# The last two column tiles of an output projection computed side by side, with the first gate weights and the seventh pair of forms prepared among their steps

## The chip, the cores and the metric

The kernel runs on one core of one Trainium2 chip. The metric is device microseconds of one execution, the median of several runs. The engines of the core are named as in the profile: PE (TensorE, the matrix unit; PEld is its loading of the stationary operand), DVE (VectorE), ACT (ScalarE), POOL (GpSimd), SP (SyncE, which here only issues transfers). Each engine has its own queue of instructions and works it off in the order in which the program was built; engines wait for each other with semaphores. A transfer (DMA) is issued by an instruction in one of these queues.

## The reference

One layer of a hybrid decoder on 512 positions of width 2048, all in float32: a norm, one input projection, eight heads of forgetting attention and eight of a compressed, selected and sliding-window attention, then an output projection with a residual, a second norm and a SwiGLU block with a residual. What matters for this change is the seam between two of these:

```
o = concatenate([o_fox, o_nsa], axis=-1) @ w_out       # 512x2048 @ 2048x2048
x = x + o                                              # x1 below
h = _rms_norm(x, ffn_norm)
x = x + (silu(h @ w_gate) * (h @ w_up)) @ w_down       # inner width 5632
```

## The kernel before, in words

All is kept transposed: a tile holds 128 of the 2048 columns on its partitions, and the 512 positions along the free axis. A float32 product is made of three products of a faster type: each operand is split into a high part (a rounded copy, made by ScalarE, line 82) and a low part (the rest, made by VectorE, line 79), and `mm3` (lines 170 to 172) adds high x high, high x low and low x high into the same bank of PSUM. The third of these needs the weights' low part; the first two need only the high one.

**The output projection.** There are 16 column tiles, in the order m = 0 to 15; tile m holds columns n = m // 2 + 8 (m % 2), so two tiles in a row are the halves of one pair. Each needs the 16 tiles `om` of the attention's result (`bigm`, two parts each) as moving operand, and 2 x 1024 columns of weights. `gemm_steps` takes them in two halves: load (`ws`, three buffers), split into high and low (`wp`, two buffers), eight steps of three matmuls. `gemm2` does two tiles at once from the same moving operand: four quarters of weights, and in each four steps of 2 x 3 matmuls. Before the change only tiles 0 and 1 go through `gemm2`.

**What follows each tile** is `x1_steps`: load the tile of x (`xr`), add the projection to it (DVE, into `x1`), store x1 in DRAM (issued by ACT), write a copy scaled by the norm's gain into `raw` (ACT), square it (ACT) and add the square to `acc` (DVE), which later gives the norm.

**Forms.** The gate and up products are computed with a scheme of Strassen's kind on 2 x 2 blocks: seven products of sums of blocks instead of eight. From each pair of x1 tiles `form_sums` makes the sums (three VectorE instructions on `raw`), `form_parts` their high and low part; there are eight such pairs of forms, and the seventh and eighth lie in `bigm`, in the place of `om` tiles 0 to 3 and 10 to 14. The weights come in groups (`fetch`: 512 KB from `wgu`; `sums`: three VectorE instructions; `parts`: a high part on ACT, a low part on DVE, each 128 x 1792), alternately into two more places of `bigm`, where `om` tiles 3 to 7 and 7 to 10 lie. A group is multiplied with two pairs of forms: 42 matmuls of 256 columns, line 1038; four groups make one tile of the gate.

**The order of the work.** A planner places instructions by priority, until `pinned` is set; from there on every instruction that goes through `tt`, `act`, `load` or `pin` keeps the order in which the source writes it. Before the change `pinned` is set in the second half of tile 15. The weights' pool `wpl` is closed behind the projection, and the pool `fpl` (with `ca`, `cb`, `cc` and the buffer `r0`) takes its place, so loads into those wait until the projection's weight buffers are free. The fetch of group 0 goes into `r0` of `fpl`, that of group 1 into `cb`.

**The end.** The down projection's last block works tile by tile of a pass (q = 0 to 3). For each it multiplies three products (`DOWN2`), one at a time, and after each calls `finish` for its next portion: the first scales and adds the third product's bank and stores one output tile; for q = 3 the other output tile is then scaled, added and stored in two halves, for the others in one piece.

Of the kernel before, what the change touches and what calls it, by code (L numbers as in the profile page):

```python
# [9 lines left out]
F32 = mybir.dt.float32  # L10
# [7 lines left out]
P = 128  # L18
D = 2048
T = 512  # L20
# [50 lines left out]
def hybrid_layer(ctx: ExitStack, tc: tile.TileContext, xT, vec, ffb, wfg, wfirst, win, cmpw, wout, wgu, wdn, out):  # L71
# [6 lines left out]
    def tt(*args, op):  # L78
        return pin(nc.vector.tensor_tensor(*args, op=op))  # L79
# [134 lines left out]

    def gemm2(os, srcs, mov, name):

        for j in range(4):
            st = wpl.tile([P, HALF * P], F32, tag="ws", name=f"ws_{name}_{j}", bufs=3)
            for i in range(2):
                load(st[:, i * T:(i + 1) * T], srcs[i][j // 2][:, j % 2 * T:(j % 2 + 1) * T])  # L220
            wp = parts_tile(f"wp_{name}_{j}")
            wp = [cut(wp, at, HALF * P) for at in (0, HALF * P)]
            split2(wp, st)
            for kk in range(4):
                k = 4 * j + kk
                for i in range(2):
                    c = slice(i * T + kk * P, i * T + (kk + 1) * P)
                    mm3(os[i], wp[0][:, c], wp[1][:, c], mov[k][:, 0, :], mov[k][:, 1, :], k == 0, k == len(mov) - 1)


    nc.scalar.dma_start(vt, vec)
# [520 lines left out]
    def x1_steps(m):  # L752
# [7 lines left out]
        tt(t, live["z"], xr, op=OP.add)  # L760
        pin(nc.scalar.dma_start(x1d[n], t))
# [12 lines left out]
    both_z = [ps.tile([P, T], F32, tag="s", name=f"po{n}", bufs=2) for n in (0, HALF)]  # L774
    gemm2(both_z, [[wout[n, 0], wout[n, 1]] for n in (0, HALF)], om, "o0")
    for m in range(NK):
        n = m // 2 + HALF * (m % 2)
        if m < 2:
            z, steps = both_z[m], iter(())
        else:  # L780
            z = ps.tile([P, T], F32, tag="g", name=f"po{n}", bufs=2)
            steps = gemm_steps(z, [wout[n, 0], wout[n, 1]], om, f"o{n}")
        x1s = x1_steps(m)
        next(x1s)
        if m == NK - 1:
            for _ in range(HALF + 1):
                next(steps)
            pinned[0] = True
        run(steps)
        live["z"] = z  # L790
        if m == NK - 1:
            break
        run(x1s)
        if m % 2 == 1:
            if m == NK - 3:
                late = live["raw"]
            else:
                form_sums(live["raw"])
                form_parts(m // 2, live["raw"])


    wst_.close()
    fpl = ctx.enter_context(tc.tile_pool(name="fpl", bufs=1, side="right", reuse_waits="tile"))

    ca = fpl.tile([P, 4, T], F32, name="ca")
    cb = fpl.tile([P, 4, T], F32, name="cb")
    cc = fpl.tile([P, 2, T], F32, name="cc")
    cslots = [ca[:, 0:2], ca[:, 2:4], cc]
    asum = cb.rearrange("p a t -> p (a t)").rearrange("p (f t) -> p f t", f=8)

    def ctile():
        cslots.append(cslots.pop(0))
# [7 lines left out]
    def fetch(i):  # L820

        if i >= 2 * NJ * NG:
            return
        if i in (1, 4):
            r = (asum if i == 1 else ca.rearrange("p a t -> p (a t)").rearrange("p (f t) -> p f t", f=8))
        else:
            pool, tag, bufs = (fpl, "r0", 1) if i == 0 or i % 3 == 2 else (ffp, "r", 2)
            r = pool.tile([P, 8, 256], F32, tag=tag, name=f"r{i}", bufs=bufs)
        raws[i] = r
        load(r[:, 0:4].rearrange("p f c -> p (f c)"), wgu[i // NG % 2, i // NG // 2, ORDER[i] % NG])  # L830
# [20 lines left out]
    def parts(i):  # L851
        run(part_steps(i))
# [56 lines left out]
    AAT = [(formx, 33 * P), (bigm, 96 * P + OFF_FORM), (bigm, 112 * P + OFF_FORM)]  # L909

    FREE = 13
    RING = [(fpl, "r0", 1), (ffp, "r", 2), (ffp, "r", 2)]
    raww, rawa, ahead = {}, {}, {}
    turn = [0, 0]

# [13 lines left out]
    def load_w(i):  # L929

        p, second, j = pass_of(i)
        u = p * NJ + j
        if not second and j < 2:
            r = cut(live["fa"], 4 * j * T, 4 * T)
        else:
            pool, tag, bufs = RING[turn[0] % 3]
            turn[0] += 1
            r = pool.tile([P, 4 * T], F32, tag=tag, name=f"wd{i}", bufs=bufs)
# [54 lines left out]
    LAST = 2 * NJ * NG - 1  # L993
    pending = iter(())
    split_w = {}
    fetch(0)
    fetch(1)
    form_sums(late)
    sums(0)
    form_parts(HALF - 2, late)  # L1000
    parts(0)
    sums(1)
    second = part_steps(1)
    next(second)
    next(x1s)
    run(second)
    for n in range(2, 5):
        fetch(n)
    for j in range(NJ):
        for which in range(2):  # L1010
            q = [ps.tile([P, T], F32, tag=tag, name=f"q{which}{j}_{i}", bufs=BUFS[tag])
                 for i, tag in enumerate(SETS[which])]
            for g in range(NG):
                i = (2 * j + which) * NG + g

                if 3 <= i < LAST - 1:
# [12 lines left out]

                for wp in range(2):  # L1030
                    for kk in range(2):
                        k = 2 * (ORDER[i] % NG) + kk
                        a = forms[k]
                        cs = slice(kk * P, (kk + 1) * P)
                        for fa, fb, b, h in PROD:
                            o = q[b][:, h * 256:(h + 1) * 256]
                            for xp in range(2 - wp):
                                nc.tensor.matmul(o, w[wp][:, fb, cs], a[:, xp, fa],  # L1038
                                                 start=(k == 0 and h == 0 and wp == 0 and xp == 0),
                                                 stop=(g == NG - 1 and kk == 1 and wp == 1), skip_group_check=True)  # L1040
                if i == 0:
                    sums(2)
                    form_sums(live["raw"])
                    parts(2)
                    sums(3)
                    form_parts(HALF - 1, live["raw"])
                elif i == 1:
                    sums(4)
                    parts(3)
                    run(x1s)  # L1050
                    fetch(5)
                elif i == 2:
# [65 lines left out]
    def finish(q, b):  # L1118
# [18 lines left out]
    TAGS = ("ss", "to", "gg", "mt")  # L1137
    for ps_ in range(4):
# [16 lines left out]
        def block(js, parts, end=None):  # L1155
# [132 lines left out]
```

## Time and profile before

| | |
|---|---|
| time, median of 3 runs | 2120.55 us (2119.72 to 2121.09) |
| the profiled execution's own time | 2121.26 us |
| its span, first to last instruction | 2119.6 us |
| TensorE busy | 2104.6 us, 99% |
| VectorE busy | 1683.5 us, 79% |
| ScalarE busy | 998.9 us, 47% |
| output projection (lines 170 to 172 on `po`) | 674.7 to 852.7 us of the span |
| gate and up products (line 1038) | from 852.7 us |

A row of the timeline is: start in microseconds from the span's start, length, engine, source line, operation, output <- input, shape, count, and in brackets how long the engine had been idle and what released it. SPq and ACTq rows are the issue of a transfer. A row of the transfers names the tile, the issuing queue, the count, the size of one and the median time from issue to landing. Line 79 is the helper through which all VectorE additions go, so it is the tile's name that tells them apart; numbers of buffers are left out of the names.

### The profile page before, as it was taken

The numbers are of one execution on the slowest core, as the hardware profiler recorded it, in microseconds if no ns is written. First come the engines' busy times: TensorE is split into PE (matmuls) and PEld (weight loads), VectorE is DVE, ScalarE is ACT, GpSimd is POOL, SyncE is SP. The second block draws the span as 40 slices with busy tenths as digits, with TensorE's granted clock in tenths as the row PEclk, the third lists the DMA queues.
The fourth block names the chain that finished last, engine by engine and source line by source line (L and its number), as shares of the span: only waits on it lengthen the run. The fifth ranks groups of instructions, "written<-read, shape, count | busy, mean of one in ns | idle before, by whom it ended". The sixth has DMA issues, their size and how long they took to land.

```text
span 2119.6 us, 38032 instructions
## 1 busy us (share of the span) xinstructions
PE 2104.6 (99%) x15667; PEld 1973.1 (93%) x15667; DVE 1683.5 (79%) x2464; ACT 998.9 (47%) x1238; POOL 188.6 (9%) x283
## 2 busy tenths in 40 slices
PE   9999999999999999999999999999999999999998
PEld 7877987888988888999999999999999999999998
DVE  6687577464566454999999999999999987889898
ACT  5455455454456343534344443343443455565554
POOL 0000000011211000111111111111111000000000
PEclk9999999999999999999999999999999999999999
DMA  5421211222222443567776776777777798479864
GB/s 195 155 70 41 70 60 47 84 86 87 95 87 71 144 149 129 164 188 209 186 199 187 185 206 182 204 184 183 206 184 197 225 337 269 151 231 332 298 176 146
DMA packets 113631, 349.64 MB, mean 165 GB/s; under 512 B 13608, under 2 KB 13864, under 8 KB 113456
## 3 DMA queue, kind: packets, MB, share of 16 engines
q1 hardware_dynamic: 85696, 270.33, 38.3%
q0 software_dynamic: 22144, 52.44, 13.7%
q10 hardware_dynamic: 5616, 24.43, 2.9%
q8 instruction: 122, 2.00, 0.4%
q14 instruction: 53, 0.43, 0.1%
HBM read 318.56 MB, written 74.73 MB: 186 GB/s over the span
## 4 chain that ended last, share of the span: by engine, by line
PE 84%; issue 10%; DVE 3%; POOL 1%; ACT 1%; DMA 0%; POOLq 0%; SPq 0%; ACTq 0%; DVEq 0%
PE q L1038 39%; PE pd L1181 13%; PE pd L1186 6%; PE po L171 3%; PE po L172 3%; PE po L170 3%; PE ps_vs L351 1%; PE ps_vf L351 1%; PE ps_qn L171 1%; PE ps_qn L172 1%; PE ps_qn L170 1%; POOL nbf L596 1%; PE ps_first L170 1%; PE ps_first L172 1%; PE ps_first L171 1%
## 5 line engine op out<-in xcount | busy, mean ns | idle before, releaser
L82 ACT ACTIVATE bigm<-r 128x1792 fp32r<-128x1792 f32 x174 | 298.3, 1714 | 467.4 <-PE q L1038 256.5
L79 DVE TENSOR_TENSOR bigm<-r,bigm 128x1792 fp32r<-128x1792 f32 x174 | 351.5, 2020 | 14.5 <-ACT bigm L82 14.1
L79 DVE TENSOR_TENSOR r<-r 128x512 f32<-128x512 f32 x522 | 267.2, 512 | 27.0 <-DMA r<-wgu 14.9
L1038 PE MATMUL q<-bigm 128*128 128x256 f32 x1848 | 217.5, 276 | 0.5 <-ACT bigm L82 0.3
L1038 PE MATMUL q<-formy,bigm 128*128 128x256 f32 x1848 | 217.0, 276 | 0.3 <-ACT bigm L82 0.3
L1038 PE MATMUL q<-formx,bigm 128*128 128x256 f32 x1848 | 217.0, 276 | 0.0
L1038 PE MATMUL q<-forma,bigm 128*128 128x256 f32 x1848 | 217.0, 276 | 0.0
L1038 PEld LDWEIGHTS q<-bigm 128*128 128x128 f32 x1848 | 213.3, 188 | 0.8 <-ACT bigm L82 0.5
L1038 PEld LDWEIGHTS q<-formy,bigm 128*128 128x128 f32 x1848 | 212.9, 188 | 0.6 <-ACT bigm L82 0.5
L1038 PEld LDWEIGHTS q<-forma,bigm 128*128 128x128 f32 x1848 | 213.2, 188 | 0.1
L1038 PEld LDWEIGHTS q<-formx,bigm 128*128 128x128 f32 x1848 | 213.0, 188 | 0.2 <-ACT bigm L82 0.2
L124 POOL DMA_DIRECT2D wsum<-wdn x176 | 119.8, 687 | 879.9 <-ACT bigm L82 775.9
L1181 PE MATMUL pd<-bigm 128*128 128x256 f32 x1200 | 148.4, 276 | 1.5 <-DVE t L79 1.5
L1181 PEld LDWEIGHTS pd<-bigm 128*128 128x128 f32 x1200 | 141.6, 188 | 1.7 <-DVE t L79 1.7
L79 DVE TENSOR_TENSOR bigm<-wd,bigm 128x1024 fp32r<-128x1024 f32 (+1 forms) x62 | 107.9, 1740 | 12.5 <-ACT bigm L82 12.3
L82 ACT ACTIVATE bigm<-rawm 128x768 fp32r<-128x768 f32 (+2 forms) x72 | 66.1, 927 | 98.4 <-PE pd L1186 63.8
L170 PE MATMUL po<-bigm,wp_o 128*128 128x512 f32 x256 | 99.7, 389 | 0.0
L171 PE MATMUL po<-bigm,wp_o 128*128 128x512 f32 x256 | 99.7, 389 | 0.0
L172 PE MATMUL po<-bigm,wp_o 128*128 128x512 f32 x256 | 99.6, 389 | 0.0
L82 ACT ACTIVATE bigm<-wd 128x1024 fp32r<-128x1024 f32 (+1 forms) x62 | 91.1, 1469 | 9.8 <-DVE wd L79 6.1
L351 PE MATMUL ps_vf<-wp_vf,bigm 128*128 128x256 f32 x768 | 95.6, 280 | 0.0
L79 DVE TENSOR_TENSOR bigm<-rawm,bigm 128x768 fp32r<-128x768 f32 (+2 forms) x72 | 75.6, 1059 | 23.7 <-ACT bigm L82 23.0
(469 smaller groups left out, 3986.0 us busy)
## 6 DMA issues: line engine op xcount, KB each, us to landing
r<-wgu SPq DMA_DIRECT2D x174, 512.0 KB, 4.4
wsum<-wdn POOLq DMA_DIRECT2D x176, 256.0 KB, 5.0
rawm<-ad SPq DMA_DIRECT2D x44, 512.0 KB, 6.8
wd<-wdn SPq DMA_DIRECT2D x40, 512.0 KB, 5.9
wd<-wsum SPq DMA_DIRECT2D x40, 512.0 KB, 6.9
ad<-cb ACTq DMA_DIRECT2D x22, 896.0 KB, 5.7
rawm<-ad SPq DMA_DIRECT2D x44, 384.0 KB, 3.3
ws_o<-wout SPq DMA_DIRECT2D x28, 512.0 KB, 3.5
```

What stands on the lines that cost most here:

```text
L79: return pin(nc.vector.tensor_tensor(*args, op=op))
L82: return pin(nc.scalar.activation(*args, **kw))
L124: d = nc.gpsimd.dma_start(step[0], step[1], **step[2])
L170: nc.tensor.matmul(o, lh, rh, start=start, stop=False)
L171: nc.tensor.matmul(o, lh, rl, start=False, stop=False)
L172: nc.tensor.matmul(o, ll, rh, start=False, stop=stop)
L351: nc.tensor.matmul(z[b][:, t * 2 * HD:(t + 1) * 2 * HD], x[:, xp, at], wp[w][:, ws], start=(c == 0 and kk == 0 and t == 0 and n == 0), sto ...
L596: nc.gpsimd.tensor_scalar(nb[:, :n], ck[:, :n], ncq[:, i, h:h + 1], 1.0, op0=OP.add, op1=OP.mult)
L1038: nc.tensor.matmul(o, w[wp][:, fb, cs], a[:, xp, fa], start=(k == 0 and h == 0 and wp == 0 and xp == 0), stop=(g == NG - 1 and kk == 1 and ...
L1181: nc.tensor.matmul(b[q][k][:, h * 256:(h + 1) * 256], w[0][:, fb, q * P:(q + 1) * P], a[xp][:, fa], start=(j == 0 and h == 0 and xp == 0), ...
L1186: nc.tensor.matmul(b[q][k][:, h * 256:(h + 1) * 256], w[1][:, fb, q * P:(q + 1) * P], a[0][:, fa], start=False, stop=(j == NJ - 1), skip_g ...
```

## The change

Tiles 14 and 15 are no longer computed one after the other: `gemm2` does both at once, in four quarters, after tile 13. `gemm2` now makes its weights one quarter ahead, and is a generator that yields after each step, for the first pair too. Ahead of the quarters stand, pinned: the loads of both x tiles, the sums of the seventh pair of forms, the fetch of gate group 0 (now into a buffer of `ffp`, which is free at that time) and its sums. After step 3 come the high and low part of the seventh forms, after step 8 those of group 0. The pool `fpl` is opened behind the pair. The x1 steps of tiles 14 and 15 both come behind it. At the end of the kernel the last block's three products go in two portions, the first alone and then the other two, and the last output tile is finished in one piece.

```diff
@@ gemm2
-        for j in range(4):
+        def weights(j):
             st = wpl.tile([P, HALF * P], F32, tag="ws", name=f"ws_{name}_{j}", bufs=3)
             for i in range(2):
                 load(st[:, i * T:(i + 1) * T], srcs[i][j // 2][:, j % 2 * T:(j % 2 + 1) * T])
             wp = parts_tile(f"wp_{name}_{j}")
             wp = [cut(wp, at, HALF * P) for at in (0, HALF * P)]
             split2(wp, st)
+            return wp
+
+        ws = [weights(0)]
+        for j in range(4):
+            if j < 3:
+                ws.append(weights(j + 1))
             for kk in range(4):
...
+                yield
@@ the projection's loop
-    for m in range(NK):
+    run(gemm2(both_z, [[wout[n, 0], wout[n, 1]] for n in (0, HALF)], om, "o0"))
+    for m in range(NK - 2):
...
-        if m == NK - 1:
-            for _ in range(HALF + 1):
-                next(steps)
-            pinned[0] = True
         run(steps)
-        live["z"] = z
-        if m == NK - 1:
-            break
         run(x1s)
-        if m % 2 == 1:
-            if m == NK - 3:
-                late = live["raw"]
-            else:
-                form_sums(live["raw"])
-                form_parts(m // 2, live["raw"])
+        if m % 2 == 1 and m < NK - 3:
+            form_sums(live["raw"])
+            form_parts(m // 2, live["raw"])
@@ fetch
-            pool, tag, bufs = (fpl, "r0", 1) if i == 0 or i % 3 == 2 else (ffp, "r", 2)
+            pool, tag, bufs = (fpl, "r0", 1) if i % 3 == 2 else (ffp, "r", 2)
@@ ahead of the gate loop
+    last_z = [ps.tile([P, T], F32, tag="g", name=f"po{n}", bufs=2) for n in (HALF - 1, NK - 1)]
+    x1a, x1b = [x1_steps(NK - 2 + i, last_z[i]) for i in range(2)]
+    next(x1a)
+    next(x1b)
+    pinned[0] = True
+    form_sums(live["raw"])
     fetch(0)
+    sums(0)
+    for k, _ in enumerate(gemm2(last_z, [[wout[n, 0], wout[n, 1]] for n in (HALF - 1, NK - 1)], om, "o7")):
+        if k == 3:
+            form_parts(HALF - 2, live["raw"])
+        elif k == 8:
+            parts(0)
+    wst_.close()
+    fpl = ctx.enter_context(tc.tile_pool(name="fpl", bufs=1, side="right", reuse_waits="tile"))
...
     fetch(1)
-    form_sums(late)
-    sums(0)
-    form_parts(HALF - 2, late)
-    parts(0)
     sums(1)
     second = part_steps(1)
     next(second)
-    next(x1s)
+    next(x1a)
     run(second)
+    next(x1b)
+    run(x1a)
...
-                    run(x1s)
+                    run(x1b)
@@ finish
-        for c in ([slice(0, 256), slice(256, T)] if q == 3 else [slice(0, T)]):
-            if c.start == 0 and q < 3:
-                yield
-            tt(t62[:, c], b[0][:, c], rstd[:, c], op=OP.mult)
-            tt(y[0][:, c], y[0][:, c], t62[:, c], op=OP.add)
-            fetch2(out[n][:, c], y[0][:, c])
-            yield
+        tt(t62, b[0], rstd, op=OP.mult)
+        tt(y[0], y[0], t62, op=OP.add)
+        fetch2(out[n], y[0])
+        yield
@@ the last block's portions
-                for some in ([[x] for x in prods] if end and ps_ == 3 else (prods,)):
+                for some in ((prods[:1], prods[1:]) if end and ps_ == 3 else (prods,)):
```

More of the change, by code (lines that the diff above doesn't have):

```diff
@@ L227, in gemm2 @@
                     c = slice(i * T + kk * P, i * T + (kk + 1) * P)
-                    mm3(os[i], wp[0][:, c], wp[1][:, c], mov[k][:, 0, :], mov[k][:, 1, :], k == 0, k == len(mov) - 1)
+                    mm3(os[i], ws[j][0][:, c], ws[j][1][:, c], mov[k][:, 0, :], mov[k][:, 1, :], k == 0, k == len(mov) - 1)
+                yield
     nc.scalar.dma_start(vt, vec)
@@ L750, in form_parts, with x1_steps @@
         split(forms[pair].rearrange("p s f t -> p s (f t)"), raw[:, 0:7].rearrange("p f t -> p (f t)"))
-    def x1_steps(m):
+    def x1_steps(m, z):
         pair, second = m // 2, m % 2
@@ L759, in x1_steps @@
         yield
-        tt(t, live["z"], xr, op=OP.add)
+        tt(t, z, xr, op=OP.add)
         pin(nc.scalar.dma_start(x1d[n], t))
@@ L774, in hybrid_layer @@
     both_z = [ps.tile([P, T], F32, tag="s", name=f"po{n}", bufs=2) for n in (0, HALF)]
-    gemm2(both_z, [[wout[n, 0], wout[n, 1]] for n in (0, HALF)], om, "o0")
-    for m in range(NK):
+    run(gemm2(both_z, [[wout[n, 0], wout[n, 1]] for n in (0, HALF)], om, "o0"))
+    for m in range(NK - 2):
         n = m // 2 + HALF * (m % 2)
@@ L782, in hybrid_layer @@
             steps = gemm_steps(z, [wout[n, 0], wout[n, 1]], om, f"o{n}")
-        x1s = x1_steps(m)
+        x1s = x1_steps(m, z)
         next(x1s)
-        if m == NK - 1:
-            for _ in range(HALF + 1):
-                next(steps)
-            pinned[0] = True
         run(steps)
-        live["z"] = z
-        if m == NK - 1:
-            break
         run(x1s)
-        if m % 2 == 1:
-            if m == NK - 3:
-                late = live["raw"]
-            else:
-                form_sums(live["raw"])
-                form_parts(m // 2, live["raw"])
[L802 to L809, printed above, removed]
+        if m % 2 == 1 and m < NK - 3:
+            form_sums(live["raw"])
+            form_parts(m // 2, live["raw"])
     def ctile():
@@ L911, in hybrid_layer @@
     FREE = 13
-    RING = [(fpl, "r0", 1), (ffp, "r", 2), (ffp, "r", 2)]
+    RING = [(0, "r0", 1), (ffp, "r", 2), (ffp, "r", 2)]
     raww, rawa, ahead = {}, {}, {}
@@ L937, in load_w @@
             turn[0] += 1
-            r = pool.tile([P, 4 * T], F32, tag=tag, name=f"wd{i}", bufs=bufs)
+            r = (pool or fpl).tile([P, 4 * T], F32, tag=tag, name=f"wd{i}", bufs=bufs)
         raww[i] = r
@@ L995, in hybrid_layer @@
     split_w = {}
-    fetch(0)
+    last_z = [ps.tile([P, T], F32, tag="g", name=f"po{n}", bufs=2) for n in (HALF - 1, NK - 1)]
[4 more added lines that the diff above has]
+    form_sums(live["raw"])
+    fetch(0)
+    sums(0)
[6 more added lines that the diff above has]
+    fpl = ctx.enter_context(tc.tile_pool(name="fpl", bufs=1, side="right", reuse_waits="tile"))
+    ca = fpl.tile([P, 4, T], F32, name="ca")
+    cb = fpl.tile([P, 4, T], F32, name="cb")
+    cc = fpl.tile([P, 2, T], F32, name="cc")
+    cslots = [ca[:, 0:2], ca[:, 2:4], cc]
+    asum = cb.rearrange("p a t -> p (a t)").rearrange("p (f t) -> p f t", f=8)
     fetch(1)
-    form_sums(late)
-    sums(0)
-    form_parts(HALF - 2, late)
-    parts(0)
     sums(1)
```

## The prediction

> **What bounds the kernel now.** I read the page first, then the waits and the timeline of each engine around the end of the output projection, then busy time by stretches, then the last 15 us.
>
> ```profile
> span 2119.6 us, 38032 instructions
> ...
> PE 2104.6 (99%) x15667; PEld 1973.1 (93%) x15667; DVE 1683.5 (79%) x2464; ACT 998.9 (47%) x1238; POOL 188.6 (9%) x283
> ```
>
> TensorE is busy for 2104.6 of 2119.6 us, and the change neither adds nor removes a matmul. So the time can move only through the 15 us in which TensorE stands, through matmuls that start late while TensorE still counts as busy, and through new gaps. The stretches behind the output projection (columns: stretch, its length, busy time and count of TensorE, of its weight load, of VectorE, ScalarE, GpSimd, then granted clock, DMA share, GB/s):
>
> ```profile
> 700.00:830.00 130.00, 130.00 (x575) 107.68 (x574) 66.27 (x74) 51.11 (x56) 0.00 (x0) 1.00 0.44 148
> 853.00:880.00 27.00, 26.24 (x219) 25.44 (x218) 24.92 (x31) 13.75 (x11) 3.83 (x7) 1.00 0.64 185
> 900.00:950.00 50.00, 50.00 (x443) 50.00 (x442) 48.98 (x67) 19.44 (x14) 8.19 (x12) 1.00 0.67 194
> 950.00:1800.00 850.00, 850.00 (x7498) 850.00 (x7497) 789.20 (x1006) 360.36 (x259) 105.48 (x155) 1.00 0.76 209
> ```
>
> A matmul of the projection starts every 130.00/575 = 0.226 us, one of the gate stage every 850.00/7498 = 0.1134 us. From 853 to 880 there are 219, worth 24.8 us at that pace: about 2.2 us are lost there. From 900 on nothing is: 443 in 50 us is the full pace, though VectorE has 48.98 of 50 us to do. So VectorE limits only the first gate groups. TensorE there (start, length, work):
>
> ```profile
> 830.70 0.39 PE L172 MATMUL po<-bigm,wp_o 128*128 128x512 f32 x1
> ...
> 852.46 0.39 PE L172 MATMUL po<-bigm,wp_o 128*128 128x512 f32 x1
> 852.68 5.11 PE L1038 MATMUL q<-forma,bigm 128*128 128x256 f32 x42
> ...
> 863.25 5.07 PE L1038 MATMUL q<-formy,bigm 128*128 128x256 f32 x42 [0.31 <-ACT bigm L82]
> 868.62 5.51 PE L1038 MATMUL q<-bigm 128*128 128x256 f32 x42 [0.31 <-ACT bigm L82]
> 873.97 5.11 PE L1038 MATMUL q<-forma,bigm 128*128 128x256 f32 x42
> ```
>
> The projection goes over into the gate without a hole (852.46, then 852.68). A group is 42 x 0.1134 = 4.76 us; the first four take 873.97 - 852.68 = 21.29 instead of 19.05, and with the fifth about 2.4 us are lost in all. That is what the change can win back here. Tile 13 of the projection, the last before the two that are paired, issues its last matmul at 830.70, so the next is due at 830.92, and there is no hole there today either.
>
> **The change part by part: the start of the pair.** In the built program each engine keeps one order of its own, and the order of the kernel before is the one the trace shows. In the changed program ScalarE has, behind tile 13: the store of x1, the scaled copy into the form buffer, the square, and only then the high half of the pair's first weights. VectorE has: the addition of x1, the addition into acc, the three sums of the seventh pair of forms, the three sums of gate group 0, and only then the low half of those weights (source order: form_sums and sums(0) stand ahead of the gemm2 loop, and all is pinned). In the kernel before the same weights' high half was made one half tile ahead. ScalarE and its queue now:
>
> ```profile
> 820.97 0.33 ACTq L761 DMA_DIRECT2D x1d<-x  x1
> ...
> 825.73 1.06 ACT L82 ACTIVATE wp_o<-ws_o 128x1024 fp32r<-128x1024 f32 x1 [3.15 <-issue]
> ...
> 831.85 0.33 ACTq L761 DMA_DIRECT2D x1d<-x  x1
> 832.22 0.73 ACT L82 ACTIVATE raw<-x,vt 128x512 f32<-128x512 f32 x1
> 832.85 0.62 ACT L82 ACTIVATE xr<-x 128x512 f32<-128x512 f32 x1
> ```
>
> The conversion at 825.73 is the one that made tile 14's first weights in time. In the changed order it follows the square, which ends at 833.47: about 833.4 to 834.45. TensorE can start the pair's first two matmuls at about 834.5, 3.6 us late. The third needs the low half. VectorE now:
>
> ```profile
> 831.12 0.69 DVE L79 TENSOR_TENSOR x<-po,xr 128x512 f32<-128x512 f32 x1 [3.07 <-PE po L172]
> ...
> 833.50 0.69 DVE L79 TENSOR_TENSOR acc<-acc,xr 128x512 f32<-128x512 f32 x1
> ...
> 837.71 1.22 DVE L79 TENSOR_TENSOR wp_o<-ws_o,wp_o 128x1024 fp32r<-128x1024 f32 x1 [3.51 <-ACT wp_o L82]
> ...
> 859.72 1.60 DVE L79 TENSOR_TENSOR r<-r 128x512 f32<-128x512 f32 x3
> 861.24 1.60 DVE L79 TENSOR_TENSOR raw<-raw 128x512 f32<-128x512 f32 x3
> 863.23 2.03 DVE L79 TENSOR_TENSOR bigm<-r,bigm 128x1792 fp32r<-128x1792 f32 x1 [0.38 <-ACT bigm L82]
> ```
>
> The addition into acc starts at 833.50 as today (it waits for the square). Three sums take 1.52 us start to start (859.72 to 861.24), the addition 0.60: form sums at 834.10, group 0's sums at 835.62, the low half at 837.15, done 1.22 later at 838.37. The third matmul starts at 838.4 instead of 830.92 + 2 x 0.226 = 831.37: **+7.0 us**, all on the path, because nothing else is in TensorE's queue. Bounds: 3.6 if the low half were ready with the high one (3.1 us of sums hidden), 7.5 if the additions overlap less than in these rows.
>
> The loads are no part of this, if they land in time. SyncE's order becomes: the x tiles of 14 and 15, group 0's gate weights, then eight half loads for the pair instead of four whole ones. The first x tile takes a buffer that the x1 store issued at 820.97 must leave, 2.5 us later (row below): 823.5. From there to the pair's first weights are 1.5 MB; at 335 GB/s that is 4.7 us, and since 512 KB take 4.4 us to land where the rate alone gives 1.6, some 2.8 more: in by about 831, 2 us ahead of ScalarE. The third weights' second half waits on a shared queue for the store issued at 831.85 (834.4), needed at 845. The fourth waits for a buffer until 838.4 and is needed at 849.
>
> ```profile
> r<-wgu SPq DMA_DIRECT2D x174, 512.0 KB, 4.4
> ...
> x1d<-x ACTq DMA_DIRECT2D x16, 256.0 KB, 2.5
> ...
> 0.00:20.00 20.00, 17.44 (x69) 13.11 (x70) 15.57 (x31) 15.57 (x26) 3.87 (x12) 1.00 0.93 335
> ```
>
> **Inside the pair.** A quarter is 24 matmuls, 5.44 us; the first ends at 838.4 + 22 x 0.226 = 843.4. Then, 0.2 later, ScalarE makes the forms' high part (1.7 us, then 1.06 for the third weights), VectorE the low ones (2.03 and 1.22): 843.6, 845.3, 847.4, 848.6, against a need at 843.4 + 5.44 + 0.45 = 849.3. Margin 0.7 us, cost nothing; if the cover goes, 0 to 0.5. The other two conversions have 3 us or more. Making the weights one quarter ahead for the first pair of tiles changes no engine's order there, so it costs nothing.
>
> **The clock.** From 831.1 to 838.4 TensorE would do two matmuls, about 0.6 us of work. What its clock does after so little is seen only at the kernel's ends (timeline of TensorE, and the last stretches, whose third figure from the right is the granted clock):
>
> ```profile
> 1.75 3.37 PE L619 MATMUL ps_warm<-ones 128*128 128x512 f32 x8 [1.75 <-DVE pc L285]
> ...
> 2117.00:2118.00 1.00, 0.00 (x0) 0.00 (x0) 0.00 (x0) 0.00 (x0) 0.00 (x0) 0.71 0.37 131
> 2118.00:2119.60 1.60, 0.00 (x0) 0.00 (x0) 0.00 (x0) 0.00 (x0) 0.00 (x0) 0.50 0.00 0
> ...
> 2112.61 0.28 PE L1186 MATMUL pd<-bigm 128*128 128x256 f32 x1
> 2114.35 0.50 PE L1181 MATMUL pd<-bigm 128*128 128x256 f32 x2 [1.47 <-DVE t L79]
> ```
>
> At the end the clock is halved from about 2117.4 on (0.71 is 0.42 us at full and 0.58 at half), 3.1 us after the last portion, nine matmuls or 1.0 us of work, had begun at 2114.35. So a stretch with 0.6 us of work in 7.3 should fall to half as well. At the start eight matmuls take 3.37 us, 0.42 each where the projection's take 0.226; that is the price of coming back: 8 x 0.195 = **+1.6 us**. Ends: 0 (it does not fall) and twice that, 3.2. I take the row.
>
> The Trainium skill, "TensorE: Matmul & The Clock Gate", section "Part 1: The HAM clock gate", puts it otherwise: the clock falls to half after a whole idle window of about 3.4 us, the windows run free, and a busy one brings it back. Read strictly, neither gap, broken by two matmuls, need hold a whole empty window, and the clock would stay; the term would be 0 and the sum 1.6 us lower. The rows at this kernel's end speak for a fall with some work in the window, so I keep the term and give the strict reading a chance of its own below.
>
> **Behind the pair.** Let E be the gate's first matmul (852.68 today, about 7 to 8.6 us later after the change). Today VectorE still has group 0's low half to make when E comes, and group 1's sums begin only at 854.4. In the new order the low half of group 0 is made in the pair's third quarter. Group 1's weights go into a buffer that the third weights leave at E - 5.24, as today (5.44 before the end, and 0.2 to release); landing takes 4.4 us, so its sums run from about E - 0.9 to E + 0.6. Then by 1.52 a sum, 2.03 a low half, 0.6 an addition, and 1.71 a high half on ScalarE:
>
> ```profile
> L82 ACT ACTIVATE bigm<-r 128x1792 fp32r<-128x1792 f32 x174 | 298.3, 1714 | 467.4 <-PE q L1038 256.5
> ```
>
> group 1 high at E + 2.4, low at 4.5, the second x1 addition and acc to 5.6, group 2's sums to 7.1, its high half at 8.9 (due 2 x 4.76 = 9.52), low 11.0, group 3's sums to 12.5, its high half at 14.2 (due 14.28), the last forms' low half at 14.4 (due 15.9), group 3's low half at 17.9, due 28 matmuls into the group, at 14.28 + 3.17 = 17.45. So some 0.5 us are still lost where 2.4 are today: **-1.9 us**. Ends: -2.4 (nothing lost) and 0 (group 1's load lands 2 us later, since three gate loads are now issued behind each other). The two x1 additions that now both follow E, and the store and copy behind each, are in this chain.
>
> **The end.** The last block's products go in two portions instead of three, and the last tile's final addition is no longer in halves. Today TensorE waits 1.47 us (row at 2114.35 above) for VectorE to read the first half of a bank before it fills the second, then VectorE does two short instructions:
>
> ```profile
> 2107.82 0.69 DVE L79 TENSOR_TENSOR t<-pd,rstd 128x512 f32<-128x512 f32 x1
> 2108.55 0.69 DVE L79 TENSOR_TENSOR cb<-cb,t 128x512 f32<-128x512 f32 x1
> ...
> 2113.88 0.42 DVE L79 TENSOR_TENSOR t<-pd,rstd 128x256 f32<-128x256 f32 x1
> ...
> 2116.16 0.42 DVE L79 TENSOR_TENSOR cb<-cb,t 128x256 f32<-128x256 f32 x1
> ...
> out<-cb SPq DMA_DIRECT2D x3, 256.0 KB, 2.0
> out<-cb SPq DMA_DIRECT2D x2, 128.0 KB, 1.7
> ```
>
> Without the wait the last nine matmuls follow 2112.61 and end at 2113.9, when VectorE is free too (2113.88). A whole multiplication and addition end at 2113.95 + 0.73 + 0.69 = 2115.37, against 2116.58 today: 1.2 earlier. The last store is 256 KB instead of 128 and lands in 2.0 instead of 1.7 us: **-0.9 us**, between -0.6 and -1.2. The other three tiles keep their instructions and order.
>
> **The sum.** 7.0 + 1.6 - 1.9 - 0.9 = +5.8 us. The profiled execution took 2121.26 (2119.6 of span and 1.66 around it), which gives 2127.1; it lies 0.71 above the median of the three runs, 2120.55, so against that the forecast is **2126.4**, 0.27% slower. About 0.2%, 4.2 us, is what a measurement of this kernel can tell from no change; the line is at 2124.8.
>
> **The rivals.** (1) The clock does not fall: 7.0 - 1.9 - 0.9 = +4.2, 2124.8, on the line. For it: the two gaps are short. Against: the rows at the end. 0.18. (It is the strict reading of the Trainium skill's page on the clock gate, named above.) (2) The stall stands, and the gain behind E does not come, because group 1's load lands late behind the pair's and beside two others: +7.7, 2128.3. For it: the third gate load in a row now takes 6.5 us to land (row below). Against: it is the first of the three in its queue, and alone it took 3.7. 0.12.
>
> ```profile
> cb<-wgu SPq DMA_DIRECT2D x1, 512.0 KB, 3.7
> ca<-wgu SPq DMA_DIRECT2D x1, 512.0 KB, 6.5
> ```
>
> (3) The sums are off the path, because VectorE does them in the 2.3 us before the square ends and in ScalarE's conversion: then only ScalarE's 3.6 us count, no fall of the clock: 3.6 - 1.9 - 0.9 = +0.8, 2121.4, no change. Against: the form sums need tile 13's copy, and VectorE's order puts acc first. 0.06. (4) Faster: the pair's first weights are ready when TensorE comes, as in the kernel before, where that conversion stood at 825.73, in the shadow of tile 13. Then nothing is lost at 830.92, and the two gains stand alone: -2.8, 2117.8. It decides from the point where the low half is ready before 831.4 + 2.8 = 834.2. For it: the buffer is free from 825.5, and all else of the change is a gain. Against: the built order of both engines. 0.06.
>
> **How the numbers follow.** The forecast's own case has 0.58 and spans 2125 to 2129.5 (clock term up to 3.2). Slower: nearly all of it, half of (1) and all of (2), 0.77. Within 0.2%: the other half of (1), (3), and a little of the main case, 0.17. Faster: (4), 0.06. (3) and (4) with 0.12 and the highest few in a hundred lie outside a range from 2124.0 ((1) with the larger gains) to 2129.2.
>
> **What would show it.** After the last matmul of tile 13 the projection's next starts about 3.6 us late, and the third about 7 us after it was due, released by VectorE's low half, with the sums of raw and r just ahead of it on VectorE. The matmuls behind it take 0.42 us each for some 3 us if the clock falls. The pair's other quarters run without holes. E comes at 859.7 to 861.3, the first four gate groups take some 19.6 instead of 21.3 us. At the end no wait before the last nine matmuls. The prediction is wrong if VectorE makes the low half before the sums, if that third matmul starts before 834, or if a later stretch, where VectorE is 98% busy, begins to hold TensorE up.

## The result, and the profile after

The changed kernel takes 2129.65 us, median of 5 runs (2128.63 to 2130.18), against 2121.09 for the kernel before, 5 runs beside it (2119.72 to 2121.42): +8.56 us, a ratio of 1.0040 with a 95% interval from 1.0028 to 1.0052. It is slower by more than a measurement of this kernel can leave open. The forecast was 2126.4 with a range up to 2129.2; the direction is right, the size is 3 us short, and the median lies 0.45 us above the range. The forecast was counted from 2120.55; the kernel before took 0.54 us more beside the change, so as a difference the forecast was +5.8 and +8.56 was measured.

The profiled execution took 2128.63 us. From the page:

```profile
span 2126.9 us, 38035 instructions
...
PE 2107.3 (99%) x15667; PEld 1974.6 (93%) x15667; DVE 1682.8 (79%) x2462; ACT 999.4 (47%) x1238; POOL 188.6 (9%) x283
```

The span grew by 7.3 us, and with the same 15667 matmuls TensorE is busy 2.7 us longer, so some of them ran slower. The rest, 4.6 us, is waits: two new ones of 6.6 us together, less some that are gone. The two new ones (work that waited and what released it; us in all, times, longest):

```profile
PE po L170 <- ACT wp_o L82: 3.4, 1, 3.4
PE po L172 <- DVE wp_o L79: 3.2, 1, 3.2
```

TensorE's timeline at the pair's start and at the transition to the gate (start, length, engine, line, work, in brackets the idle time before it and what ended it):

```profile
831.94 0.39 PE L172 MATMUL po<-bigm,wp_o 128*128 128x512 f32 x1
835.70 0.50 PE L170 MATMUL po<-bigm,wp_o 128*128 128x512 f32 x1 [3.38 <-ACT wp_o L82]
836.04 0.40 PE L171 MATMUL po<-bigm,wp_o 128*128 128x512 f32 x1
839.66 0.79 PE L172 MATMUL po<-bigm,wp_o 128*128 128x512 f32 x1 [3.23 <-DVE wp_o L79]
840.25 0.63 PE L170 MATMUL po<-bigm,wp_o 128*128 128x512 f32 x1
840.68 0.63 PE L171 MATMUL po<-bigm,wp_o 128*128 128x512 f32 x1
...
862.79 5.11 PE L1046 MATMUL q<-forma,bigm 128*128 128x256 f32 x42
867.74 5.10 PE L1046 MATMUL q<-formx,bigm 128*128 128x256 f32 x42
872.68 4.92 PE L1046 MATMUL q<-formy,bigm 128*128 128x256 f32 x42
877.76 3.56 PE L1046 MATMUL q<-bigm 128*128 128x256 f32 x28 [0.16 <-ACT bigm L82]
```

Tile 13 issues its last matmul at 831.94. The pair's third was due three steps of 0.227 later, at 832.62, and starts at 839.66: 7.04 us late. What VectorE did meanwhile:

```profile
832.37 0.69 DVE L79 TENSOR_TENSOR x<-po,xr 128x512 f32<-128x512 f32 x1 [7.81 <-PE po L172]
834.73 0.69 DVE L79 TENSOR_TENSOR acc<-acc,xr 128x512 f32<-128x512 f32 x1 [1.68 <-ACT xr L82]
835.34 1.60 DVE L79 TENSOR_TENSOR raw<-raw 128x512 f32<-128x512 f32 x3
836.87 1.60 DVE L79 TENSOR_TENSOR r<-r 128x512 f32<-128x512 f32 x3
838.39 2.35 DVE L79 TENSOR_TENSOR wp_o<-ws_o,wp_o 128x1024 fp32r<-128x1024 f32 x2
```

and ScalarE:

```profile
834.09 0.61 ACT L82 ACTIVATE xr<-x 128x512 f32<-128x512 f32 x1
834.61 1.99 ACT L82 ACTIVATE wp_o<-ws_o 128x1024 fp32r<-128x1024 f32 x2
```

The chain is in these rows: square (`xr`), high half (`wp_o`) on ScalarE; addition into acc, three sums on `raw`, three on `r`, low half on VectorE; then the third matmul. The rows behind it are 0.43 us apart where 0.227 is the pace: the clock is at half. The stretches (busy time and count of TensorE, weight load, VectorE, ScalarE, GpSimd; then granted clock, DMA share, GB/s):

```profile
831.00:838.00 7.00, 2.06 (x8) 1.05 (x6) 3.85 (x7) 3.14 (x4) 0.00 (x0) 0.89 0.50 183
838.00:839.00 1.00, 0.00 (x0) 0.00 (x0) 0.96 (x3) 0.00 (x0) 0.00 (x0) 0.50 0.00 0
...
843.00:844.00 1.00, 1.00 (x6) 0.77 (x5) 0.00 (x0) 0.00 (x0) 0.00 (x0) 0.84 0.01 2
844.00:845.00 1.00, 1.00 (x6) 0.84 (x5) 0.00 (x0) 1.00 (x1) 0.00 (x0) 1.00 0.00 0
```

The granted clock is a mean over the stretch, as a share of the full clock. A granted 0.89 over 7 us is 1.54 us at half (2 x 0.11 x 7), so it fell at 836.46; 0.84 over the last one is 0.32 us at half, so it was back at 843.32.

At the end the wait ahead of the last nine matmuls is gone; the last of TensorE, of VectorE and of SyncE:

```profile
2122.13 0.28 PE L1190 MATMUL pd<-bigm 128*128 128x256 f32 x1
...
2123.17 0.69 DVE L79 TENSOR_TENSOR cb<-cb,t 128x512 f32<-128x512 f32 x1
...
2123.89 0.33 SPq L906 DMA_DIRECT2D out<-cb  x1
```

Four points cut an execution: the first matmul on `po`, E (the gate's first matmul), the first on `pd`, the end of the span. The table is worked out from their starts in each trace (for the change 675.91, 862.79, 1702.86 and 2126.9). The kernel before was profiled three times, the change twice.

| kernel | first po at | po to E | E to pd | pd to end |
|---|---|---|---|---|
| before, first | 674.68 | 178.00 | 841.67 | 425.20 |
| before, second | 675.60 | 178.02 | 841.01 | 425.20 |
| before, third | 676.82 | 178.04 | 840.38 | 425.19 |
| changed, first | 675.91 | 186.88 | 840.06 | 424.07 |
| changed, second | 676.58 | 188.01 | 839.81 | 424.07 |

All of the loss is between the projection's start and E: +8.9 and +10.0 us. Behind E the change wins, 1.1 us at the end in every execution, and between 0.3 and 1.9 in the gate, depending on which executions are compared. The first column is work that the change does not touch; it differs by 2 us between executions of one kernel. The clock has a part in that: in the two executions with the latest first po, the third of the kernel before and the second of the changed one, it is at half for 3.4 us from about 85.2 (0.50 granted from 85.19 to 88.60 in the former), where the other three have 1.00.

### The profile page after: what moved, and what is told of

Its sections match the earlier page's. It is cut to its first block, busy times and chain, and to the rows that moved or that the text cites. A ratio compares the mean times of both kernels' runs of the same rounds, so it can differ in the third digit from the quotient of the medians.

```text
span 2126.9 us, 38035 instructions
## 1 busy us (share of the span) xinstructions
PE 2107.3 (99%) x15667; PEld 1974.6 (93%) x15667; DVE 1682.8 (79%) x2462; ACT 999.4 (47%) x1238; POOL 188.6 (9%) x283
## 4 chain that ended last, share of the span: by engine, by line
PE 84%; issue 10%; DVE 3%; POOL 1%; ACT 1%; DMA 0%; POOLq 0%; ACTq 0%; SPq 0%; DVEq 0%
PE q L1046 39%; PE pd L1185 13%; PE pd L1190 6%; PE po L172 3%; PE po L171 3%; PE po L170 3%; PE ps_vs L358 1%; PE ps_vf L358 1%; PE ps_qn L171 1%; PE ps_qn L172 1%; PE ps_qn L170 1%; POOL nbf L603 1%; PE ps_first L170 1%; PE ps_first L172 1%; PE ps_first L171 1%
## 5 line engine op out<-in xcount | busy, mean ns | idle before, releaser
L172 PE MATMUL po<-bigm,wp_o 128*128 128x512 f32 x256 | 100.5, 393 | 3.2 <-DVE wp_o L79 3.2
```

The lines of the kernel that those rows point to most:

```text
L172: nc.tensor.matmul(o, ll, rh, start=False, stop=stop)
```

## The experiments

The theory is that of the prediction: the pair's first weights are late because their conversions stand behind the sums (VectorE) and the scaled copy and square (ScalarE), and a clock at half adds to it. The rivals left are that the clock has no part in it, that the preparation among the steps is worth nothing or costs, and that what is missing in the forecast lies in the gate or at the end.

**The sums one step later.** Both sets of sums and the fetch are moved behind the pair's first step:

```diff
-    form_sums(live["raw"])
-    fetch(0)
-    sums(0)
     for k, _ in enumerate(gemm2(...)):
-        if k == 3:
+        if k == 0:
+            form_sums(live["raw"])
+            fetch(0)
+            sums(0)
+        elif k == 3:
```

> The changed kernel with the form sums, the fetch and the sums of gate group 0 moved behind the pair's first step; all else as in the changed kernel. Theory (VectorE's order sets the stall): VectorE makes the low half of the first weights right behind acc, so the pair's third matmul is about 4.4 us late instead of 7.0 (ScalarE's high half, 3.6, and 1.2 for the low half less what overlaps). With the gains of the gate's first groups (1.6) and the end (1.2): 1.6 us over the kernel before if the clock stays, up to 5.0 if it falls. Rival (the loads or ScalarE set the stall): the third matmul as late as in the changed kernel, about 8.6 us over the kernel before.

Measured: 2125.72 us (2123.81 to 2127.55, 11 runs) against 2121.32 for the kernel before on the same chip, ratio 1.0018 (1.0010 to 1.0027), +4.40 us, inside the 1.6 to 5.0 expected. TensorE's timeline and its stretches:

```profile
836.44 0.50 PE L170 MATMUL po<-bigm,wp_o 128*128 128x512 f32 x1 [3.37 <-ACT wp_o L82]
...
837.70 0.79 PE L172 MATMUL po<-bigm,wp_o 128*128 128x512 f32 x1 [0.38 <-DVE wp_o L79]
```

```profile
831.00:838.00 7.00, 3.25 (x13) 1.97 (x12) 2.96 (x4) 3.13 (x4) 0.00 (x0) 0.92 0.58 218
838.00:844.00 6.00, 6.00 (x22) 4.85 (x22) 3.69 (x7) 1.70 (x1) 0.00 (x0) 0.81 0.33 95
```

The wait for the low half shrinks from 3.23 to 0.38 us, and the third matmul is 4.34 us late instead of 7.04: the sums ahead of the low half are worth 2.7 us; the rest is ScalarE's high half and the low half that can only follow it. The clock still falls, but for less long: 0.92 over 7 us is 0.56 us at half and 0.81 over 6 is 1.14 lost, which is 2.28 at half; so from 836.88 to 840.28, 3.4 us. From po to E it takes 183.66; less the 178.02 of the kernel before and the stall of 4.34, 1.3 us remain for the clock.

**The weights early.** The sums stay one step later, and beside that the pair's first quarter of weights is loaded and converted under tile 13, ahead of its x1 steps, as the kernel before did for tile 14:

```diff
+        if m == NK - 3:
+            last_w = [[wout[n, 0], wout[n, 1]] for n in (HALF - 1, NK - 1)]
+            first = quarter(last_w, "o7", 0)
         run(x1s)
...
-        ws = [weights(0)]
+        ws = [first or quarter(srcs, name, 0)]
```

> As the run before it, and the pair's first quarter of weights is also loaded and split under tile 13, ahead of that tile's x1 steps. Theory: no stall at the pair's start but about 0.3 us for a PSUM bank, the clock stays full, and only the two gains are left: 2.5 us under the kernel before. Rival (something ahead of the pair has become slower by 1.2 us, as the one profile of the changed kernel shows): 1.3 us under it. Rival (the pair as such costs time): not below the kernel before.

Measured: 2119.68 us (2118.66 to 2120.84, 11 runs), ratio 0.9991 (0.9982 to 0.9999): 1.64 us faster than the kernel before, where 2.5 had been expected, and 10 under the changed one (measured on another chip). The same stretch as above:

```profile
831.00:838.00 7.00, 7.00 (x32) 5.54 (x31) 3.17 (x4) 2.20 (x3) 0.00 (x0) 1.00 0.57 207
```

TensorE is busy through it at full clock. From po to E it takes 178.23, the 178.0 of the kernel before. So the pair itself costs nothing, nor does the work among its steps: the whole loss ahead of E is the late start, with what the clock does behind it. The expectation's rival, that something ahead of the pair has become slower, is not borne out: the first po is at 676.43 here, inside the 674.68 to 676.82 of the kernel before. What falls short is the gate: E to pd takes 840.40, against 840.38 to 841.67.

**The end alone.** The kernel before, with only the last block's two portions and the last tile finished in one piece (the last two parts of the change's diff).

> The kernel before with the change of the last block and the last output tile alone. Theory: TensorE's wait of 1.47 us goes, the last store is issued 1.2 us earlier and its 256 KB land 0 to 0.3 us later than 128 KB: 0.9 to 1.2 us under the kernel before. Rival (the last store's size eats it): no difference.

Measured: 2120.67 us (2119.12 to 2121.79, 11 runs), ratio 0.9996 (0.9987 to 1.0005), 0.65 us under the median of before, where 0.9 to 1.2 had been expected. The interval takes in no change; the trace tells more, since from pd to the end it takes 424.31 instead of 425.20, 0.9 less. This execution also gave a reading that was not looked for. Its seam is that of the kernel before, yet from E to pd it takes 840.11, nearly what the changed kernel takes. Group 0's load is issued and its sums start here at

```profile
845.05 0.33 SPq L85 DMA_DIRECT2D r<-wgu  x1
...
848.67 1.61 DVE L79 TENSOR_TENSOR r<-r 128x512 f32<-128x512 f32 x3 [1.64 <-DMA r<-wgu]
```

and in the first profile of the kernel before at

```profile
844.35 0.33 SPq L85 DMA_DIRECT2D r<-wgu  x1
...
848.95 1.15 DVE L79 TENSOR_TENSOR r<-r 128x512 f32<-128x512 f32 x2 [2.63 <-DMA r<-wgu]
```

From issue to sums 3.62 and 4.60 us, for the same 512 KB. That is taken up below.

This kernel is also what the one with the weights early has to be set against, since both have the new end. By the medians of the same chip the pair wins 1.0 us more (2119.68 against 2120.67). The two traces do not show that gain: from po to the end they take 1442.7 and 1442.4 us, and the first is the slowest of its 11 runs, the second among the fastest of its own. So the 1.0 us is read from the times alone, and the stage in which it is won is not shown.

**The gap filled.** The changed kernel with 27 matmuls of 512 columns added between tile 13 and the pair, into a bank of their own that nothing reads, so that TensorE is busy while it waits. This is added work, and the result does not use it:

```diff
+    fill = ps.tile([P, T], F32, tag="m", name="ps_fill")
+    for i in range(27):
+        pin(nc.tensor.matmul(fill, ones, om[0][:, 0, :], start=(i == 0), stop=(i == 26)))
     form_sums(live["raw"])
```

> The changed kernel with 27 idle matmuls of 512 columns into an unused PSUM bank between tile 13 and the pair, 6.1 us of work that ends before the low half is ready. Theory (the clock falls to half in the gap and stays there for 4 to 7 us): the pair's third matmul is as late as before, 7.0 us, but the clock stays full: 1.8 to 3.4 us under the changed kernel, its runs closer together, mean granted clock 0.999 as before the change. Rival (the clock costs nothing beyond what one profile shows, the rest is elsewhere): as the changed kernel less 1.8. Rival (idle matmuls only add work): not below the changed kernel.

Measured: 2126.24 us (2125.33 to 2127.28, 11 runs), ratio 1.0021 (1.0012 to 1.0030), so +4.92 us over the kernel before. TensorE's timeline and the stretch behind:

```profile
831.89 6.28 PE L993 MATMUL ps_fill<-bigm,ones 128*128 128x512 f32 x27
...
839.39 0.74 PE L172 MATMUL po<-bigm,wp_o 128*128 128x512 f32 x2 [0.31 <-DVE wp_o L79]
```

```profile
838.00:844.00 6.00, 5.69 (x25) 4.37 (x24) 2.47 (x3) 1.70 (x1) 0.00 (x0) 1.00 0.29 87
```

The low half comes as late as before, and the clock stays at 1.00. The kernel with 27 matmuls more is faster than the one without: +4.92 against +8.56, and +7.95 in the next run, so 3.0 to 3.6 us less. Of these 0.45 are not the clock: in this build the first two matmuls of both tiles come ahead of the first that needs the low half (two L172 in one row above), so four instead of two are done by then. That leaves 2.6 to 3.2 us for the clock; by the traces' stretch from po to E (184.81 against 186.88 and 188.01, less 0.45) 1.6 and 2.75.

**The changed kernel and the kernel before again.** Both unchanged, profiled on one more chip, since the sum and the stages had been read from one execution of each. The kernel before was profiled twice there.

> The changed kernel once more, for a second profile and more runs. Theory (the half clock ends only with a window of the clock's monitor, whose phase is chance): po starts and stalls as in the first profile (third matmul 7.0 us late), but the matmuls at half clock run for another length, between 1.5 and 5 us or more, and the median is again 8 to 9 us over the kernel before. Rival (the median lies above the first profile by chance of the runs): 7.4 us over it.

> The kernel before once more, for a second profile of its seam. Theory (the 2.4 us lost in the first gate groups of the first profile hung on group 0's load, which landed 1 us later there than in the run of the end alone): with a landing of some 3.6 us the first four groups take about 20.3 us instead of 21.3, and the change has next to nothing to win there. Rival (2.4 us are the rule, the run of the end alone was lucky): 21.3 again.

> The kernel before a third time, for the same question: the first four gate groups take 20.3 us where group 0's load lands in about 3.6 us, 21.3 where it takes 4.6.

Measured: changed 2128.99 us (2128.50 to 2130.88, 5 runs) against 2121.04 (15 runs), ratio 1.0039 (1.0026 to 1.0051), +7.95 us; the two single executions of the kernel before took 2121.52 and 2122.13. The stages are in the table above. The changed kernel's start of the pair, TensorE's timeline and stretches:

```profile
836.37 0.80 PE L170 MATMUL po<-bigm,wp_o 128*128 128x512 f32 x1 [3.38 <-ACT wp_o L82]
...
840.33 0.80 PE L172 MATMUL po<-bigm,wp_o 128*128 128x512 f32 x1 [2.74 <-DVE wp_o L79]
```

```profile
831.00:838.00 7.00, 3.22 (x11) 1.81 (x9) 3.22 (x6) 3.13 (x4) 0.00 (x0) 0.86 0.54 201
838.00:844.00 6.00, 3.67 (x9) 2.90 (x10) 3.34 (x5) 0.00 (x0) 0.00 (x0) 0.50 0.27 87
844.00:848.00 4.00, 4.00 (x14) 3.21 (x13) 0.00 (x0) 1.70 (x1) 0.00 (x0) 0.71 0.00 0
```

The stall is the same 7.04 us: the third matmul was due 0.67 later than in the first execution, as the first po is, and starts 0.67 later. The clock is not the same: at half from 836.04 (0.86 over 7 us) to 846.32 (0.71 over 4 is 2.32 at half), 10.3 us instead of 6.9. From po to E, less 178.02 and 7.04, it cost 2.95 us here and 1.82 in the first execution.

In the third profile of the kernel before, group 0's load, its sums, and the gate's first and fifth group:

```profile
846.52 0.33 SPq L85 DMA_DIRECT2D r<-wgu  x1
...
850.42 1.61 DVE L79 TENSOR_TENSOR r<-r 128x512 f32<-128x512 f32 x3 [1.93 <-DMA r<-wgu]
```

```profile
854.86 5.11 PE L1038 MATMUL q<-forma,bigm 128*128 128x256 f32 x42
...
875.40 4.92 PE L1038 MATMUL q<-forma,bigm 128*128 128x256 f32 x42
```

The load takes 3.90 us from issue to sums, and the first four groups take 20.54 us, where the execution the prediction read took 21.29. Set beside each other:

| profile of | issue to group 0's sums | first four groups | E to pd |
|---|---|---|---|
| before, first | 4.60 | 21.29 | 841.67 |
| before, second | 4.36 | 21.01 | 841.01 |
| before, third | 3.90 | 20.54 | 840.38 |
| before with the new end | 3.62 | 20.26 | 840.11 |
| changed, first | ahead of the pair | 20.21 | 840.06 |
| changed, second | ahead of the pair | 19.96 | 839.81 |

The issue stands 8.3 us ahead of E in all four of the upper rows. What the first four groups lose follows the landing of that one load, 1.03 us for 0.98; the second profile, with 4.36 and 21.01, lies between the two cases that were expected for it. The prediction had read the latest landing of the four.

**Nothing among the steps.** The kernel with the weights early, but all preparation behind the pair; only the fetch stays ahead of it:

```diff
     fetch(0)
+    run(gemm2(last_z, last_w, om, "o7", first))
+    form_sums(live["raw"])
+    form_parts(HALF - 2, live["raw"])
     sums(0)
-    for k, _ in enumerate(gemm2(...)):
-        ...
+    parts(0)
```

> The kernel with the weights early (the one that was 1.6 us under the kernel before), but the seventh forms' sums and parts and group 0's sums and parts all behind the pair's last step instead of among the steps. Theory: VectorE comes to group 0's sums some 3 us before the gate instead of 15, group 1's sums begin 2.2 us behind the gate's first matmul instead of 0.5 ahead of it, and the first gate groups lose about 2 us more: about 0.4 us over the kernel before. Rival (the work among the steps is worth nothing, VectorE has room either way): as the kernel with the weights early, 1.6 under.

Measured: 2123.10 us (2121.85 to 2124.47, 11 runs), ratio 1.0009 (1.0000 to 1.0018), +2.06 us over the kernel before, where 0.4 had been expected. From po to E it takes 178.46, and the first four groups 22.67 instead of the 20.55 with the preparation among the steps. VectorE, and the third group on TensorE:

```profile
851.84 1.60 DVE L79 TENSOR_TENSOR r<-r 128x512 f32<-128x512 f32 x3
...
857.16 1.60 DVE L79 TENSOR_TENSOR cb<-cb 128x512 f32<-128x512 f32 x3
```

```profile
855.24 5.05 PE L1047 MATMUL q<-forma,bigm 128*128 128x256 f32 x42
...
867.25 5.06 PE L1047 MATMUL q<-formy,bigm 128*128 128x256 f32 x42 [1.52 <-ACT bigm L82]
```

Here group 1's sums come 1.9 us behind E, and TensorE waits for the groups' parts. So the preparation among the steps is worth 3.4 us by the medians (2123.10 and 2119.68, on different chips), 3.7 if each is set against the kernel before beside it, and 2.7 from po to pd in the two traces. About 2 had been expected. So in the paired kernel this work belongs among the steps; with that and an early start the pair is no slower than two tiles one after the other, and the start as written undoes that.

## Why the prediction was right or wrong

**What bounds the kernel.** Right: matmuls, and TensorE alone. The loss is two waits of TensorE and matmuls at half clock, with no new stretch later at which VectorE holds it up (E to pd is shorter than before, not longer).

**The start of the pair, +7.0.** Right in size and in each link: 7.04 us in both executions, the first matmul 3.5 us late (due 832.17, started 835.70), released by ScalarE's high half where 3.6 was forecast, the third released by VectorE's low half, with acc, the sums of `raw` and the sums of `r` ahead of it in that order. The experiments carry it as cause: the sums moved away take 2.7 us of it, the weights moved ahead as well take the rest.

**The loads and the inside of the pair, nothing.** Right: both waits at the start are for conversions and not for loads, and with the weights early the pair takes no more than two tiles one after the other. The 0.7 us of margin held.

**The clock, +1.6 with ends 0 and 3.2.** Right that it falls, mis-sized in the value: 1.8 and 2.95 us by the stages of two executions, 2.6 to 3.2 by the medians with the gap filled. The step that failed is "that is the price of coming back: 8 x 0.195": eight warm-up matmuls were all there was to slow down at the start, whereas here work stood ready for as long as the clock stayed low. In the first execution TensorE worked at half clock from 839.66 to 843.32, which loses half of 3.66 us, 1.8; in the second from 840.33 to 846.32, 3.0, because its clock came back one stretch later. The bound of 3.2 was good, the value taken should have been nearer to it. Rival (1), no fall, is refuted by the granted clock.

The strict reading of the Trainium skill ("TensorE: Matmul & The Clock Gate", section "Part 1: The HAM clock gate"), which would have kept the clock, does not hold here. In the experiment with the sums one step later there was a single gap, from 833.07 (the end of tile 13's last matmul) to 836.44, which is 3.37 us, and the clock fell at 836.88 with 0.44 us of work behind the gap. The page's length of a window, about 3.4 us, does agree: 3.4, 6.9 and 10.3 us at half are one, two and three of these.

**Behind the pair, -1.9 with ends -2.4 and 0.** Mis-sized, and the step that failed is the first one, "2.4 us are lost there today". That was true of the one execution that had been read, the one in which group 0's load took longest. Between the first profiles of both kernels the gain is 1.6; over the three profiles of the kernel before and the one with the new end (mean E to pd 840.8) it is 0.9. The changed kernel's side was also a little too good: the first four groups take 20.2 and 20.0 instead of the 19.6 forecast. Group 1's sums start 0.5 us ahead of E where 0.9 was forecast. And not all of the 2.4 us was waiting for VectorE: in the changed kernel the first two groups take 4.95 and 4.94 us without a wait (the rows at 862.79, 867.74 and 872.68), so a matmul starts every 0.118 us there and not every 0.1134, and the fifth group that the prediction counted, from 21.29 to 26.24 us behind E, does the same. What slows these matmuls is not shown. Less these 0.37 us of the first two groups the changed kernel loses 0.8 and 0.5 us, against the 0.5 forecast. Rival (2), that this gain would not come, had the mechanism wrong (the load lands in time) and the number nearer: +7.7.

**The end, -0.9 with ends -0.6 and -1.2.** Right: -1.13 by the trace in both executions, -0.9 and by medians -0.65 where it stands alone. No wait is left ahead of the last nine matmuls.

**Rivals (3) and (4).** Refuted for the change. The case of (4), weights ready in time, was built: -1.64 measured where -2.8 was named, short by about what the gate's gain was overrated (1.0).

**The sum.** 7.04, then 1.8 to 3.0 for the clock, 0.9 and 1.1 won, is +6.8 to +8.0, against +8.0 and +8.6 by the medians. Both errors of size went the same way, which put the median over the range. What remains, 0 to 1.8 us, is within the 2 us by which executions of one kernel differ ahead of the projection; it was not resolved further. Between the first profiles alone the stages from po on give +6.1 (8.88 - 1.61 - 1.13), close to the forecast of +5.8; that is in part luck, since this pair has the smaller price of the clock and the latest landing.

## What to carry to other kernels

When work is put ahead of a step, look at what that step's own first operands wait for: here six small sums and two small copies stood ahead of the two conversions that TensorE waited for, and converting one tile earlier, with the sums behind the first step, turned +8 us into -1.6. A stall of TensorE has a second price in matmuls at half clock; it depends on when the stall falls, so take it as a range worked out from whole stretches at half clock and not from the few matmuls seen at a kernel's start. A gain that rests on a transfer having landed late should be read from more than one execution.

## What the runs showed of the hardware that had not been expected

The clock stays at half for whole multiples of one length: 3.4, 6.9 and 10.3 us. If stretches of 3.4 us are laid back from each fall, the stretch that led to the fall had 0.44 us of matmuls in it with the sums one step later (13%) and about 0.74 (22%) in the changed kernel's first execution, so a little work does not keep the clock up. The other way round, a stretch with one gap of 0.38 us (89% busy) brought it back, and one with TensorE busy from 840.33 to 842.9 (75%) did not. No experiment was made on where the limits lie, but the traces narrow them, at a place that the change does not touch. In the third profile of the kernel before the stretch from 81.78 to 85.19 has 1.74 us of matmuls in it (51%, the longest gap 1.37 us) and the clock is at half for the 3.41 us behind it; in the changed kernel's first profile the stretch from 82.19 to 85.60 has 1.91 us (56%) and the clock stays. Nor is the busy share all that decides: near the end of the run without preparation a stretch with 1.64 us (48%, 2116.05 to 2119.46) keeps the clock.

27 matmuls that compute nothing of use made the kernel 3.0 to 3.6 us faster, 2.6 to 3.2 of it because they kept the clock.

One load of 512 KB, issued at the same point of the program, took between 3.6 and 4.6 us from issue to the work it releases in four executions, and the gate's first groups followed it.
